# Two moves around layer A's attention in a two-layer decoder trunk: the third pair's loads go behind the last gate product, and a one-column exponential goes among the last projection products

## The chip, the cores and the metric

One core of a Trainium2 chip runs the whole kernel. The metric is device time in microseconds (us), the median of the runs of one kernel. Engines are named as the profile names them: PE (TensorE matmul), PEld (its weight loads), DVE (VectorE), ACT (ScalarE), POOL (GpSimd) and SP (SyncE, which here issues nearly all DMAs).

## The reference, cut to what matters

```python
# layer A (x: 2048 x 1024, 16 heads of 64)
u = rmsnorm(h, norm_a_g);  proj = u @ w_in_a
q, k, v, f_logit, gate = split(proj)              # q, k normed per head
o = fox_attention(q, k, v, log_sigmoid(f_logit + b_forget))   # causal softmax with a forget bias
h = h + (o * silu(gate)) @ w_out_a
# then shared K/V from rmsnorm(h), and layer B: sliding-window attention with sinks,
# again h + (o * silu(gate)) @ w_out_b
```

## The kernel before, in words

Every product with weights is made of three matmuls on pairs of high and low parts (`h`, `lo`), so that it is close to fp32. The core works through four stages: the projections of layer A (`projections`), the attention of layer A (`attention_a`), the output projection (`out_a`), and layer B.

`projections` goes through groups of columns of `w_in_a`; for each block of 128 rows 24 matmuls (L804) fill a PSUM tile `b2` (the trace says `b`), and ACT reads it out (L572 for v, with DVE's L573 behind it). In the last group (the second half of v) the hook runs `attention_a`'s generator a step further between matmuls: 40 such steps (`EARLY`) each put one piece of the row maxima (L982) among the projection products, and step 3 (`REST_AT`) loads the rest of head 0.

`attention_a` then takes steps of two key blocks: scores on PE (L1027, L1028, and masks in L1033 and L1037), exponential on ACT (L1043 or L1034), its split into a high part (ACT, L1046) and a low part (POOL, L1047), sums on DVE (L1056), and the products with v (L1071, in the PSUM tile `pa`). Among these steps PE gets "filler": the gate projection, one matmul (L1117) at a time from the generator `gate`. A gate product is a PSUM tile of 128 features x 512 rows, made of 24 matmuls; its operands are eight pairs of tiles `wh` and `wl`, which hold the normed input of 512 rows, and two tiles of split weights, each 512 KB, loaded from the DRAM scratch `wg` (L1093) into tiles of the tag `wr` (two buffers) or, at the end, alternately of `st` (four buffers) and `wr`. Behind each product come DVE L1129, ACT L1130 (tanh), DVE L1131, and a store to `gt` (L1132). The last 60 matmuls of the filler are kept for the end of attention: 12 finish a product in the bank `pb`, 24 make the next-to-last product in a bank of `mx`, and 24 make the last product in `pb` again. Between them stand the last values' output (L1081, stores to `om` and `oc`) and the reciprocal of the last row sums (`recips`: PE L953, DVE L959 and L960, a store to `rd`).

`out_a` consumes "pairs": a pair is a tile of 128 rows of `o * silu(gate)`, transposed, for two heads and 512 positions. Its four inputs (`om`, `oc`, `gt` and the reciprocal sums `rd`, 256 KB each) are loaded by `gated_load` (L1246 to L1251). For the first three pairs these go to tiles of the tags `qn` (two buffers), `wh`, `qn` and `wl`; for the later ones to `wh`, `wl`, `wh`, `wl`. A pair is then prepared: for pairs 0 and 1 by five operations on POOL (L1263), for the later ones by POOL L1274, DVE L1275 and L1278, ACT L1279 and DVE L1280. Step s of `out_a` is 24 matmuls (L1320) with pair s; `op.step(s)` prepares pair s + 2 and loads up to pair s + 5. Steps 0 and 1 come first for six of the eight bank halves and then for the last two, so step 2 begins behind 48 matmuls.

What sets the order: the code is written in one sequence, and a scheduler with priorities and its own time estimates then orders each engine's instructions; those pinned with `keep_in_program_order` keep their place. A DMA waits at the head of SP's queue for the data or the buffer it needs and holds back every DMA behind it. Buffers are handed round within a tag. The kernel divides PSUM into eight banks; `attention_a` uses `sc` (3), `mx` (2), `pa`, `pb` and `ac`, and `out_a` lays its own tiles over the same banks.

Where ACT goes over to a function of another table, an `ACT_TABLE_LOAD` stands ahead of it in the trace. `constants` makes a one-column tile `warm` and applies a square root to it.

Of the kernel before, what the change touches and what calls it, by code (L numbers as in the profile page):

```python
# [17 lines left out]
AF = mybir.ActivationFunctionType  # L18
# [5 lines left out]
P = 128  # L24
# [45 lines left out]

MAX_AT = 5
EARLY = 40
REST_AT = 3

IDLE = 22
# [28 lines left out]
def f_(ap):  # L104
    return ap.bitcast(F32)
# [57 lines left out]
class Trunk:  # L163
# [57 lines left out]
    def constants(self):  # L221
        nc, cp, a = self.nc, self.const, self.a

        def select(view, src, pattern, base, cm, fill):
            nc.gpsimd.affine_select(
                out=view, in_=src, pattern=pattern, compare_op=ALU.is_ge,
                fill=fill, base=base, channel_multiplier=cm,
            )

        def tile_(name, shape, dt=F32):  # L230
            return cp.tile(shape, dt, name=name, tag=name)

        idle = self.sb("sq", [P, CH], F32R)
        nc.vector.memset(f_(idle), 0.0)
        ps = self.ps("pb", [P, CH])
        for i in range(IDLE):
            self.tc.keep_in_program_order(
                nc.tensor.matmul(ps, idle[:, :P], idle, start=i == 0, stop=i == IDLE - 1)
            )

        self.ones = tile_("ones", [P, P])
        nc.gpsimd.memset(self.ones, 1.0)
        self.tri = tile_("tri", [P, P])
        select(self.tri, self.ones, [[1, P]], 0, -1, 0.0)
        self.ident = tile_("ident", [P, P])
        select(self.ident, self.tri, [[-1, P]], 0, 1, 0.0)

        self.fold = tile_("fold", [P, 32])
        nc.vector.tensor_tensor(self.fold, self.ident[:, :32], self.ident[:, 32:64], ALU.add)
        for c in (64, 96):  # L250
            nc.vector.tensor_tensor(self.fold, self.fold, self.ident[:, c : c + 32], ALU.add)
        nc.vector.tensor_single_scalar(self.fold, self.fold, 2.0, ALU.mult)
        self.identb = tile_("identb", [P, P], BF16)
        nc.vector.tensor_copy(self.identb, self.ident)

        self.mask_s = tile_("mask_s", [P, P], BF16)
        nc.gpsimd.memset(self.mask_s, 0.0)
        select(self.mask_s, self.mask_s, [[1, P]], 0, -1, NEG)

        self.band = tile_("band", [P, 2, P], BF16)  # L260
        nc.gpsimd.memset(self.band[:, 0], 0.0)
        select(self.band[:, 0, :], self.band[:, 0, :], [[-1, P]], 0, 1, NEG)
        nc.vector.tensor_tensor(self.band[:, 1], self.tri, self.ident, ALU.subtract)

        self.loads = []
        warm = tile_("warm", [P, 1])
        nc.scalar.activation(warm, self.ones[:, :1], AF.Sqrt)

        def vector(name, n, views):
            t = tile_(name, [P, n])  # L270
            for rows, src in views:
                self.loads.append((t[rows], src))
            return t

        def column(name, src, n):
            return vector(name, n, [(slice(0, P), src.rearrange("(t p) -> p t", p=P))])

        def pair_column(name, src):
            col = src.rearrange("(p o) -> p o", o=1)
            return vector(name, 1, [(slice(0, HD), col), (slice(HD, P), col)])  # L280

        def row(name, src, n):
            return vector(name, n, [(slice(0, P), src.to_broadcast([P, n]))])

        self.g_a = column("g_a", a["norm_a_g"][0], NDT)
        self.bf = row("bf", a["b_forget"], H)
        self.g_qa = pair_column("g_qa", a["qnorm_a_g"][0])
        self.g_ka = pair_column("g_ka", a["knorm_a_g"][0])
        self.g_b = column("g_b", a["norm_b_g"][0], NDT)
        self.g_kv = column("g_kv", a["kv_norm_g"], NDT)  # L290
        self.g_qb = pair_column("g_qb", a["qnorm_b_g"][0])
        self.g_kb = pair_column("g_kb", a["knorm_b_g"])
        self.sink = row("sink", a["sinks"], H)
        self.gq16 = row("gq16", a["qnorm_b_g"][:, :ROT], ROT)
# [601 lines left out]
    def attention_a(self, op):  # L896


        nc, tc, d = self.nc, self.tc, self.d
# [28 lines left out]
        def load_rest(h):  # L928
            kq = self.sb("big", [P, 2, S], F32R)
            nc.sync.dma_start(out=f_(kq[:, 0, :]), in_=d["ka"][h])  # L930
            nc.sync.dma_start(out=f_(kq[:, 1, :]), in_=d["qa"][h])
            if h % 2 == 0:
                v2 = self.sb("big", [P, 2, NTB, P], F32R)
            else:
                v2 = heads[h - 1][5]
            v = v2[:, h % 2]
            nc.sync.dma_start(out=f_(v), in_=d["va"][h].rearrange("(n p) e -> p n e", p=P))
            heads[h][0], heads[h][2] = kq[:, 0, :], kq[:, 1, :]
            heads[h][4:] = v, v2
# [218 lines left out]
        def ahead(target):  # L1158
            nonlocal done
            while done < min(target, len(pieces)):  # L1160
                pieces[done]()
                done += 1

        for n in range(EARLY):
            yield
            if n == REST_AT:
                load_rest(0)
            ahead(n + 1)
        yield
        pht, plt = self.sb("big", [P, 4, 1024], F32R), self.sb("big", [P, 4, 1024], F32R)  # L1170
# [53 lines left out]
                next(parts)  # L1224
        for _ in op.prepare_parts(1):
            pass
        op.load(2, ("qn", "wh", "qn", "wl"))
        for item, more in zip(pending, HELD):
            feed(fed + more)
            values(item, pin=more > 0)  # L1230
# [6 lines left out]
            op.weight_split(p)  # L1237
        for _ in filler:
            pass


    def gated_load(self, ch, p, tiles):
# [479 lines left out]
```

## Time and profile before

| | |
|---|---|
| median of 3 runs | 2425.08 us (2423.46 to 2425.10) |
| the profiled execution | 2422.62 us |
| its span, first to last instruction | 2420.9 us |
| granted TensorE clock, mean | 0.998 |
| PE busy | 2398.9 us, 99% of the span |
| DVE, ACT, POOL busy | 1731.5, 1259.7, 999.5 us |

The span is shorter than the profiled execution's own time by 1.7 us, which lie around it. Times in the views count from the start of the span. In a row of the timeline stand start, duration, engine, source line, operation, output tile and input tiles; the bracket at the end is the idle time of the engine before this row and what ended it. The rows of the DMA queue (SPq) are the issues, not the transfers. Attention of layer A runs from about 591 to 1449 us, `out_a` from 1449 to 1626 us.

### The profile page before, as it was taken

What the parts mean: (1) busy time and instruction counts of PE and PEld (TensorE: products, weight loads), DVE (VectorE), ACT (ScalarE), POOL (GpSimd) and SP (SyncE); (2) the same over time, 40 slices, a digit from 0 to 9 for tenths busy, and PEclk for the clock granted to TensorE, in tenths of its full rate; (3) what the DMA queues carried; (4) which work ended last, traced back from release to release, by engine and by line L of the source; (5) the groups of instructions that cost most, each with busy time, mean ns of one, the idle gap of its engine ahead of it and who ended that gap; (6) DMA issues with size and microseconds to landing.
All of it is one profiled execution on the core that took longest, in us unless ns stands there. A gap on an engine that the chain in (4) does not pass through costs nothing.

```text
span 2420.9 us, 36284 instructions
## 1 busy us (share of the span) xinstructions
PE 2398.9 (99%) x11960; PEld 2027.5 (84%) x11960; DVE 1731.5 (72%) x4086; ACT 1259.7 (52%) x2502; POOL 999.5 (41%) x644
## 2 busy tenths in 40 slices
PE   9999999999999999999999989999999999999999
PEld 7888899988888888888888868888888888888887
DVE  7756667735898998988989855456766643677775
ACT  5433324323878778878878751135423322466664
POOL 0000000011877777877877862210011000388885
PEclk9999999999999999999999999999999999999999
DMA  6656555677654755575476549975434484765652
GB/s 189 204 170 190 155 152 170 196 230 233 189 159 124 223 135 172 146 228 158 115 215 162 148 131 314 298 261 150 133 97 126 149 265 143 234 219 181 183 183 74
DMA packets 357004, 436.03 MB, mean 180 GB/s; under 512 B 65296, under 2 KB 248624, under 8 KB 350640
## 3 DMA queue, kind: packets, MB, share of 16 engines
q1 hardware_dynamic: 348464, 403.30, 55.3%
q10 hardware_dynamic: 8352, 30.41, 4.3%
q8 instruction: 95, 1.56, 0.3%
q14 instruction: 93, 0.76, 0.1%
HBM read 273.69 MB, written 159.79 MB: 179 GB/s over the span
## 4 chain that ended last, share of the span: by engine, by line
PE 95%; DMA 2%; DVE 1%; POOL 1%; ACT 1%; issue 0%; SPq 0%; POOLq 0%; ACTq 0%
PE b L804 30%; PE pa L1071 10%; PE pb L1549 7%; PE pb L1117 7%; PE sc L1027 5%; PE b L1320 5%; PE sc L1028 5%; PE mx L982 5%; PE b L766 4%; PE b L1403 3%; PE pa L1488 2%; PE pb L766 2%; PE fl L368 1%; PE pa L368 1%; PE pb L368 1%; PE pa L766 1%
## 5 line engine op out<-in xcount | busy, mean ns | idle before, releaser
L804 PE MATMUL b<-wh,big 128*128 128x512 f32 (+3 forms) x2560 | 772.3, 374 | 1.1 <-DVE big L405 0.6
L1047 POOL TENSOR_TENSOR big<-st,big 128x1024 fp32r<-128x1024 f32 (+1 forms) x320 | 657.7, 2077 | 236.5 <-ACT big L1046 162.4
L804 PEld LDWEIGHTS b<-wh,big 128*128 128x128 f32 x2560 | 470.6, 188 | 72.8 <-ACT wh L515 2.5
L804 PE MATMUL b<-wl,big 128*128 128x512 f32 (+3 forms) x1280 | 473.7, 370 | 1.2 <-DVE wl L516 1.1
L1056 DVE TENSOR_TENSOR ac<-ac,st 128x512 f32<-128x512 f32 (+3 forms) x576 | 353.2, 613 | 32.7 <-ACT ac L1050 14.2
L1043 ACT ACTIVATE st<-sc 128x512 f32<-128x512 f32 (+1 forms) x512 | 274.6, 583 | 109.9 <-PE sc L1028 46.2
L1071 PE MATMUL pa<-big 128*128 128x512 f32 (+3 forms) x1280 | 318.5, 365 | 0.8 <-POOL big L1047 0.6
L1046 ACT CAST big<-st 128x1024 fp32r<-128x1024 f32 (+1 forms) x320 | 294.8, 922 | 8.1
L804 PEld LDWEIGHTS b<-wl,big 128*128 128x128 f32 x1280 | 241.3, 189 | 37.2 <-DVE wl L516 5.2
L1071 PEld LDWEIGHTS pa<-big 128*128 128x128 f32 x1280 | 228.9, 190 | 37.1 <-POOL big L1047 1.9
L1027 PE MATMUL sc<-big 128*128 128x512 f32 (+3 forms) x640 | 233.6, 369 | 0.1
L995 DVE TENSOR_REDUCE mt<-mx 128x1 f32<-128x384 f32 (+1 forms) x360 | 214.2, 598 | 27.0 <-PE mx L982 24.6
L524 ACT ACTIVATE sq<-b,r 128x512 f32<-128x512 f32 (+2 forms) x128 | 77.7, 607 | 298.0 <-PE b L804 298.0
L1028 PE MATMUL sc<-big 67*128 67x512 f32 (+3 forms) x640 | 229.2, 367 | 0.0
L982 PE MATMUL mx<-big 66*128 66x512 f32 (+2 forms) x600 | 225.4, 379 | 0.0
L526 DVE TENSOR_REDUCE sm<-sq 128x8 f32<-128x512 f32 (+2 forms) x128 | 74.8, 584 | 138.6 <-ACT sq L524 138.4
L906 POOL MEMSET rot<- 128x512 bf16 x1 | 0.5, 524 | 418.8 <-PE pb L368 418.8
L1117 PE MATMUL pb<-wh,wr 128*128 128x512 f32 x488 | 171.3, 394 | 0.0
L1451 POOL TENSOR_TENSOR big<-big,tri 128x1024 fp32r<-128x1024 f32 x60 | 144.1, 2402 | 61.0 <-DVE big L1448 61.0
L990 DVE CUSTOM_DVE_ANT_0 mx<-mx,rot 128x384 f32<-128x384 f32 (+2 forms) x240 | 147.6, 620 | 27.9 <-PE mx L982 25.2
L1027 PEld LDWEIGHTS sc<-big 128*128 128x128 f32 x640 | 121.5, 190 | 22.6 <-ACT st L1043 1.1
L539 POOL TENSOR_TENSOR ro<-qn,rot 128x64 f32<-128x64 f32 (+1 forms) x48 | 15.6, 325 | 296.4 <-DVE qn L530 290.8
(289 smaller groups left out, 4229.4 us busy)
## 6 DMA issues: line engine op xcount, KB each, us to landing
wr<-wg ACTq DMA_DIRECT2D x58, 512.0 KB
va<-st SPq DMA_DIRECT2D x32, 512.0 KB
ka<-st SPq DMA_DIRECT2D x64, 256.0 KB
ut<-big SPq DMA_DIRECT2D x16, 1024.0 KB
big<-ka SPq DMA_DIRECT2D x16, 1024.0 KB
big<-qa SPq DMA_DIRECT2D x16, 1024.0 KB
qb<-st SPq DMA_DIRECT2D x64, 256.0 KB
big<-qb SPq DMA_DIRECT2D x16, 1024.0 KB
```

Of the source, the lines that this page charges most:

```text
L766: nc.tensor.matmul(ps, W[k][dt][:, ft * P : (ft + 1) * P], u[ch][:, dt, :], start=(dt == 0 and i == 0), stop=(dt == NDT - 1 and i == 2),)
L804: nc.tensor.matmul(ps[:, :n], u[tb // 4][:, dt, us], W[k][dt], start=(dt == 0 and i == 0), stop=(dt == NDT - 1 and i == 2),)
L982: mm = nc.tensor.matmul(ps, qb[:66, i * P : (i + 1) * P], kb[:66, k0:k1], start=True, stop=True,)
L995: nc.vector.reduce_max(o, ps, axis=AX.X)
L1027: nc.tensor.matmul(o, ka[:, ks], qa[:, qs], start=not (last and n_), stop=False)
L1028: nc.tensor.matmul(o, kb[:, ks], qb[:, qs], start=False, stop=not diag)
L1043: nc.scalar.activation(pf[:, off : off + w], ps[:, :w], AF.Exp, scale=HD**-0.5)
L1046: nc.scalar.copy(ph[:, :tw], pf[:, :tw])
L1047: nc.gpsimd.tensor_tensor(pl[:, :tw], pf[:, :tw], f_(ph[:, :tw]), ALU.subtract)
L1056: nc.vector.tensor_tensor(a_, a_, pf[:, off : off + w], ALU.add)
L1071: product = nc.tensor.matmul(pv[:, q0 : q0 + w], v[:, k, :], src[:, off : off + w], start=(p == 0 and n_ == 0 and i == 0), stop=(last and ...
L1117: nc.tensor.matmul(ps, w[:, dt // 2 % 2, wk, dt % 2, :], us[dt][uk], start=(dt == 0 and i == 0), stop=(dt == NDT - 1 and i == 2),)
```

## The change

A load of the third pair (`op.load(2, ...)`, five DMAs) moves from ahead of the last products of attention to behind the last gate product; and in step 20 of the 40 early steps a one-column exponential on `warm` is issued and pinned, among the last projection products. `warm` becomes an attribute for that. Nothing that reaches the output is computed otherwise.

```diff
+EXP_AT = 20
...
-        warm = tile_("warm", [P, 1])
-        nc.scalar.activation(warm, self.ones[:, :1], AF.Sqrt)
+        self.warm = tile_("warm", [P, 1])
+        nc.scalar.activation(self.warm, self.ones[:, :1], AF.Sqrt)
...
             if n == REST_AT:
                 load_rest(0)
+            if n == EXP_AT:
+                exp = nc.scalar.activation(self.warm, self.ones[:, :1], AF.Exp)
+                tc.keep_in_program_order(exp)
             ahead(n + 1)
...
         for _ in op.prepare_parts(1):
             pass
-        op.load(2, ("qn", "wh", "qn", "wl"))
         for item, more in zip(pending, HELD):
             feed(fed + more)
             values(item, pin=more > 0)
         gate_bank, weight_slots = "mx", cycle(["st", "wr"])
         feed(fed + 3 * NDT)
         gate_bank = "pb"
         for _, args in due:
             recips(*args)
         for p in range(PAIRS_READY):
             op.weight_split(p)
         for _ in filler:
             pass
+        op.load(2, ("qn", "wh", "qn", "wl"))
```

Since the scheduler orders the instructions, the diff doesn't show the new order. Lines of the kernel before stand one to four lower in the changed one (L1093 is L1094, L1132 is L1133, L1246 is L1250, L1275 is L1279). First SP's queue at the end of attention, from the third last load of gate weights (`wr<-wg`) to the store of the last reciprocal sums or beyond; before:

```order
L1093 DMA wr<-wg 128x1024
L1093 DMA st<-wg 128x1024
L1247 DMA wh<-oc 128x512
L1251 DMA wl<-rd 64x512
L1246 DMA qn<-om 128x512
L1248 DMA qn<-gt 128x512
L1251 DMA wl<-rd 64x512
L1083 DMA om<-sq 64x512
L1132 DMA gt<-sq 128x512
L1084 DMA oc<-sq 64x512
L1093 DMA st<-wg 128x1024
L1093 DMA wr<-wg 128x1024
```

and the same place of the changed kernel, up to the third pair's last load:

```order
L1094 DMA wr<-wg 128x1024
L1094 DMA st<-wg 128x1024 x2
L1094 DMA wr<-wg 128x1024
L1084 DMA om<-sq 64x512
L1085 DMA oc<-sq 64x512
L1133 DMA gt<-sq 128x512
L1250 DMA qn<-om 128x512
L1251 DMA wh<-oc 128x512
L1252 DMA qn<-gt 128x512
L1255 DMA wl<-rd 64x512
L962 DMA rd<-sq 48x32
L1255 DMA wl<-rd 64x512
```

The last two loads of gate weights stood behind the third pair's five loads and three stores; they now stand ahead of all of them.

Then DVE behind the next-to-last gate product (whose bank is `mx`), up to the third pair's last operation; `sq_15306`/`sq_15298` belong to the last gate product, `qn_15190`/`qn_15303` to the third pair, `wh_15322`/`wh_15323` to the fourth. Before:

```order
L1129 TENSOR_TENSOR sq_15306<-pb_15277,rows_13561 128x512
L1275 TENSOR_TENSOR wh_15322<-wh_15322,wl_15325 128x512
L1131 SCALAR_TENSOR_TENSOR sq_15306<-sq_15306,pb_15277 128x512
L1275 TENSOR_TENSOR qn_15190<-qn_15190,wl_15193 128x512
L1278 TENSOR_TENSOR wh_15322<-wh_15322,wh_15324 128x512
L1278 TENSOR_TENSOR qn_15190<-qn_15190,qn_15192 128x512
L1280 TENSOR_TENSOR big_14360<-wh_15322,big_14360 128x512
L1280 TENSOR_TENSOR big_14360<-qn_15190,big_14360 128x512
```

and now:

```order
L1130 TENSOR_TENSOR sq_15298<-pb_15269,rows_13562 128x512
L1132 SCALAR_TENSOR_TENSOR sq_15298<-sq_15298,pb_15269 128x512
L1279 TENSOR_TENSOR qn_15303<-qn_15303,wl_15306 128x512
L1282 TENSOR_TENSOR qn_15303<-qn_15303,qn_15305 128x512
L1279 TENSOR_TENSOR wh_15323<-wh_15323,wl_15326 128x512
L1284 TENSOR_TENSOR big_14361<-qn_15303,big_14361 128x512
```

The third pair still comes behind the last gate product; one operation of the fourth pair, which waits for that pair's loads, stands ahead of the third pair's last.

Last ACT at the step from the projections (L572, each on the next tile `b2`) to attention (L1043); before:

```order
L572 ACTIVATE st_5576<-b2_5529,r_144 128x8x64
L572 ACTIVATE st_5620<-b2_5580,r_144 128x8x64
L572 ACTIVATE st_5664<-b2_5624,r_144 128x8x64
L572 ACTIVATE st_5713<-b2_5668,r_144 128x8x64
L1043 ACT_TABLE_LOAD
L1043 ACTIVATE st_5726<-sc_5724 128x512
```

and now:

```order
L1170 ACT_TABLE_LOAD
L1170 ACTIVATE warm_132<-ones_108 128x1
L573 ACTIVATE st_5577<-b2_5529,r_144 128x8x64
L573 ACTIVATE st_5621<-b2_5581,r_144 128x8x64
L573 ACTIVATE st_5665<-b2_5625,r_144 128x8x64
L573 ACTIVATE st_5714<-b2_5669,r_144 128x8x64
L1044 ACTIVATE st_5727<-sc_5725 128x512
```

The table load stands four projection products earlier, and none is left ahead of attention's first exponential.

## The prediction

> **What bounds the kernel now.** I read the page first, then the waits of PE, then the timelines of the two places that the change touches. The page's rows of busy time:
>
> ```profile
> span 2420.9 us, 36284 instructions
> PE 2398.9 (99%) x11960; PEld 2027.5 (84%) x11960; DVE 1731.5 (72%) x4086; ACT 1259.7 (52%) x2502; POOL 999.5 (41%) x644
> ```
>
> PE is busy for 99% of the span, so a change that leaves the matmuls alone can only win what PE waits or runs slowly. The waits of PE, the longest and the two that matter beside it (total, times, longest):
>
> ```profile
> PE pb L1117 <- DMA st<-wg: 11.3, 1, 11.3
> ...
> PE b L804 <- DVE big L405: 0.6, 1, 0.6
> PE pa L1071 <- POOL big L1047: 0.6, 2, 0.4
> ```
>
> One wait of 11.3 us is most of what PE loses: the last gate product waits for its first weights. SP's timeline tells why they came late:
>
> ```profile
> 1419.45 0.33 SPq L1093 DMA_DIRECT2D wr<-wg  x1
> 1419.89 0.36 SPq L1093 DMA_DIRECT2D st<-wg  x1
> 1426.81 0.32 SPq L1247 DMA_DIRECT2D wh<-oc  x1
> ...
> 1431.77 0.33 SPq L1246 DMA_DIRECT2D qn<-om  x1
> 1433.11 0.32 SPq L1248 DMA_DIRECT2D qn<-gt  x1
> 1433.48 0.48 SPq L1251 DMA_DIRECT2D wl<-rd  x1
> ...
> 1434.69 0.54 SPq L1132 DMA_DIRECT2D gt<-sq  x1
> ...
> 1435.83 1.44 SPq L1093 DMA_DIRECT2D st<-wg  x1
> 1437.36 0.38 SPq L1093 DMA_DIRECT2D wr<-wg  x1
> ...
> 1452.20 0.54 SPq L1246 DMA_DIRECT2D wh<-om  x1
> ```
>
> From 1420.3 to 1435.8 the queue holds the third pair's loads, and three of them go out right behind an operation of pair 1 on POOL, whose buffers they need (the last row quoted is the first load of pair 5, used further down):
>
> ```profile
> 1417.12 7.43 POOL L1047 TENSOR_TENSOR big<-st,big 128x1024 fp32r<-128x1024 f32 x3 [0.48 <-ACT big L1046]
> 1424.52 2.27 POOL L1263 TENSOR_TENSOR qn<-qn,wh 128x512 f32<-128x512 f32 x1
> ...
> 1430.48 1.26 POOL L1263 TENSOR_TENSOR qn<-qn 128x512 f32<-128x512 f32 x1
> 1431.82 1.26 POOL L1263 TENSOR_TENSOR big<-qn,big 128x512 fp32r<-128x512 f32 x1
> ```
>
> L1247 follows the operation that ends at 1426.79, L1246 the one that ends at 1431.74, L1248 the one that ends at 1433.08. The gate weights need none of these; they only stand behind. PE's rows there:
>
> ```profile
> 1423.86 0.40 PE L1117 MATMUL pb<-wh,wr 128*128 128x512 f32 x1
> ...
> 1424.89 0.44 PE L1117 MATMUL mx<-wh,st 128*128 128x512 f32 x1
> ...
> 1430.52 0.28 PE L953 MATMUL sc<-fold,part 128*48 128x32 f32 x2
> 1442.09 0.76 PE L1117 MATMUL pb<-wh,st 128*128 128x512 f32 x1 [11.30 <-DMA st<-wg]
> ...
> 1448.98 8.32 PE L1320 MATMUL b<-big 128*128 128x512 f32 x36
> ...
> 1459.86 4.24 PE L1320 MATMUL b<-big 128*128 128x512 f32 x18
> ...
> 1465.30 4.24 PE L1320 MATMUL b<-big 128*128 128x512 f32 x18
> ```
>
> **Term 1, the wait.** In the changed order both loads of last gate weights stand ahead of the third pair. The `st` load follows its predecessor at once: of the four `st` buffers it takes the one of the third last attention step, whose POOL reader is the first of the three L1047 from 1417.12; a third of 7.43 us later is 1419.6. So it goes out at about 1420.3. The chain of waits shows what such a load took with others around it:
>
> ```profile
> 1435.83 6.13 DMA st<-wg
> ```
>
> At 6.13 us it lands by 1426.4, and PE wants it at 1430.8, when L953 ends. The `wr` load waits for the matmul at 1423.86, goes out at 1424.3 and lands by 1430.4; its 12 matmuls begin half a product later, at 1433.5. The bank `pb` must be read out first, which DVE's L1131 ends at 1429.86 (row below). All 11.30 us go.
>
> **Term 2, the clock.** The windows (length, busy times by engine, granted clock, DMA share, GB/s) of the last gate product, of the products behind it, and of a long stretch of the output projection:
>
> ```profile
> 1442.10:1449.00 6.90, 6.90 (x25) 5.60 (x26) 0.00 (x0) 0.00 (x0) 1.28 (x1) 0.79 0.74 218
> 1449.00:1454.40 5.40, 5.40 (x25) 4.49 (x24) 5.13 (x7) 1.45 (x3) 1.62 (x1) 1.00 0.70 200
> ...
> 1459.90:1481.00 21.10, 21.10 (x95) 17.48 (x94) 11.65 (x15) 5.32 (x7) 4.40 (x3) 1.00 1.03 346
> ```
>
> After its wait PE runs the product at a granted clock of 0.79 on the mean. Its 24 matmuls take 1448.98 - 1442.09 = 6.89 us; 24 of the output projection take 1465.30 - 1459.86 = 5.44. Without the wait there is no reason for the slow clock: 1.45 us more. [...]
>
> **Term 3, crowding.** The earlier `st` load now flies beside the two issued at 1419.45 and 1419.89, and PE takes the second of these at 1424.89. The window of those two:
>
> ```profile
> 1419.90:1424.40 4.50, 4.39 (x20) 3.29 (x19) 4.43 (x6) 3.25 (x5) 4.50 (x2) 1.00 0.72 235
> ```
>
> They move 235 x 4.5 = 1.06 MB and so end by about 1424.4. Shared evenly, 0.52 MB more at the 346 GB/s of a saturated stretch take 1.5 us, so the next-to-last product could wait until 1425.7, 0.8 us. Served in turn it waits not at all. I take 0.2 us of loss, near the end without a wait, since two loads issued 0.44 us apart already landed in time for PE here. [...]
>
> **Term 4, the exponential.** ACT and PE at the start of attention, and windows there:
>
> ```profile
> 591.65 0.69 ACT L572 ACTIVATE st<-b,r 128x512 fp32r<-128x512 f32 x1 [6.02 <-PE b L804]
> 592.36 1.28 ACT L1043 ACT_TABLE_LOAD   x1
> 593.65 0.60 ACT L1043 ACTIVATE st<-sc 128x512 f32<-128x512 f32 x1
> ...
> 590.00:600.00 10.00, 9.39 (x45) 7.11 (x45) 4.02 (x10) 8.32 (x14) 3.84 (x3) 1.00 0.83 250
> ```
>
> The table load of 1.28 us stands ahead of the first exponential and so of the split, POOL's part and the first products with v. But PE has other matmuls: of these 10 us it lacks 0.61, 0.4 of it in the wait for POOL. The gain is bounded by 0 and 0.61; the scheduler also moves a few gate matmuls here, so I take the middle, 0.3. The load's new place costs nothing: the last L572 finds ACT idle for 6.02 us, as long as a projection product takes, and 1.28 us and one column of exponential fit. If that cover were gone, PE would be late by at most 1.3 us.
>
> **What else is moved.** The stores to `om`, `oc` and `gt` go out ahead of the third pair, when their data is there. The third pair's loads still wait for POOL: L1250 at 1431.8, L1252 at 1433.1. Behind them stands the new neighbour, the store of the last reciprocal sums, and the third pair's last load is queued behind that. DVE's rows:
>
> ```profile
> 1429.17 0.69 DVE L1131 SCALAR_TENSOR_TENSOR sq<-sq,pb 128x512 f32<-128x512 f32 x1 [0.70 <-ACT sq L1130]
> 1438.47 0.69 DVE L1129 TENSOR_TENSOR sq<-mx,rows 128x512 f32<-128x512 f32 x1 [8.62 <-DMA gt<-sq]
> ...
> 1454.86 0.69 DVE L1280 TENSOR_TENSOR big<-qn,big 128x512 fp32r<-128x512 f32 x1
> ```
>
> The `gt` store issued at 1434.69 released DVE at 1438.47, 3.8 us. Issued at 1429.9 it releases its buffer by 1433.7, and the reciprocals follow to 1434.3; then go the `rd` store, the last `rd` load at 1434.8 and, from 1435.7, pair 3. The output projection can start at 1448.98 - 12.75 = 1436.2. Pair 2 is needed 10.88 us later (1459.86 - 1448.98), at 1447.1. DVE does the last gate product's part to about 1438.7, then pair 2 and, ahead of its last operation, one of pair 3, whose last load is issued at 1438.5. At 3.8 us of landing this ends about 1443.5; at 6.13 about 1446. Before, it ended at 1455.55, 4.3 us early; now 1 to 3.6. No wait, but the cover is thin. For the later pairs the loads come some 2.5 us later against PE than before (pair 5: issued 3.2 us behind the projection's start, now 5). Their cover before, by the two rows with the least of it that I found:
>
> ```profile
> 1487.34 1.63 DVE L1280 TENSOR_TENSOR big<-wh,big 128x512 fp32r<-128x512 f32 x1 [0.69 <-ACT big L1279]
> ...
> 1496.69 1.46 DVE L1280 TENSOR_TENSOR big<-wh,big 128x512 fp32r<-128x512 f32 x2
> ```
>
> Steps 9 and 10 begin at 1459.86 + 7 x 5.44 = 1497.9 and at 1503.4; their pairs end at 1489.0 and 1497.4, so 9 and 6 us remain, and about 6 and 3.5 after the change. At the start of layer B DVE's L405 goes ahead of two operations of the projection's end, and ACT's order changes; PE's wait of 0.6 for that L405 can go or grow to about twice that: 0, with 0.6 either way.
>
> **The sum**: 11.30 + 1.45 - 0.2 + 0.3 = 12.85 us. The profiled execution took 2422.62 us, of which 1.7 lie around the span; it would take 2409.8. It was 2.46 us faster than the median, so I forecast 2425.08 - 12.85 = 2412.2 us, 0.53% less.
>
> **Rivals.** (a) Pair 2 comes late, and a part of the wait moves into the output projection. For it speaks DVE's new order, behind a load of pair 3; against it the 1 to 3.6 us left. If DMAs there take 10 us, pair 2 ends near 1450 and PE waits 3 us: 2415. If later pairs lose their cover too, say 3 us more, 2418. (b) The output projection falls to the pace of its loads, and the time ends on the other side: the loads of pairs 2 to 4 flew during the wait, and behind it DMA is full (share 1.03). Three pairs of 1.05 MB at 346 GB/s are 9 us, which leaves 3.9 us of gain; it is slower than before only from 12.85 us of loss, and by 0.2% from 17.7, which is six pairs' loads with no cover at all: 2430. Against it stand 6 to 9 us of cover and three pairs, not six. (c) The change doesn't do what it says: the gate weights still land late, because a buffer or the crowd holds them. Only a landing time above 10.5 us for `st` (1420.3 to 1430.8) or 9.2 for `wr` makes PE wait; at 12 us some 3 us return: 2415. (d) The exponential does nothing: 2412.5, within the range.
>
> **How the numbers follow.** Forecast with (d) 0.82, (a) 0.10, (c) 0.04, (b) 0.04, of which slower than before 0.015. The forecast's own range is the sum with its ends: gain 11.30 + 1.45 - 0.8 + 0 - 0.6 = 11.35 to 11.30 + 1.45 + 0.6 + 0.6 = 13.95, so 2411.1 to 2413.7; the three runs differ by 1.6 us, and the profiled one lies lower still, so 2409.5 to 2415. For 8 in 10 I add most of (a): 2409 to 2417. A difference under 0.2% (4.85 us) can't be told from none; all of the forecast and most of (a) and (c) lie beyond it: faster 0.95, same 0.03, slower 0.02.
>
> **What the changed profile would show.** PE's wait for `st<-wg` gone, the clock 1.00 through the last gate product, the output projection starting at about 1436, `st<-wg` issued twice in a row near 1420, no `ACT_TABLE_LOAD` between 592 and 594, and L1320 without a gap. A wait of PE on DVE's L1284 at step 2, or of the next-to-last gate product for `st<-wg`, would show terms wrong; a gap in steps 9 to 12 would show (b).

## The result: 12.4 us faster, as forecast, with a small loss in the output projection

The changed kernel takes 2412.66 us (median of 5 runs, 2411.01 to 2414.55) against 2425.08 for the kernel before (5 runs, 2422.65 to 2426.01). The ratio is 0.995, 95% interval 0.9937 to 0.9963, so 9 to 15 us less. The forecast was 2412.2. Measured a second time, beside new runs of the kernel before, it took 2411.59 against 2423.43 (ratio 0.9948, 0.9936 to 0.996).

Here is the changed kernel's profile. First the page's span and busy times, then PE's waits (total, times, longest):

```profile
span 2408.8 us, 36281 instructions
PE 2399.6 (100%) x11960; PEld 2026.4 (84%) x11960; DVE 1732.4 (72%) x4086; ACT 1260.6 (52%) x2503; POOL 1000.6 (42%) x644
...
PE pb L239 <- DVE sq L235: 1.5, 1, 1.5
PE pa L426 <- DVE ro L413: 0.7, 2, 0.4
PE b L1324 <- DVE big L150: 0.7, 1, 0.7
```

PE's busy time is 0.7 us longer and the span 12.1 us shorter, so in sum what went is waiting. (The last gate product got 1.31 us shorter, as worked out further down, but PE's busy time in the output projection grew by 0.88 us and that at the head of attention by 0.5.) The wait for `st<-wg` is gone. One in the list is new, 0.7 us for DVE's L150 (the low part of a block of the output projection's weights). SP's timeline at the end of attention:

```profile
1418.69 0.33 SPq L1094 DMA_DIRECT2D wr<-wg  x1
1419.13 1.12 SPq L1094 DMA_DIRECT2D st<-wg  x2
1423.52 0.32 SPq L1094 DMA_DIRECT2D wr<-wg  x1
...
1429.12 0.33 SPq L1133 DMA_DIRECT2D gt<-sq  x1
1431.02 0.33 SPq L1250 DMA_DIRECT2D qn<-om  x1
...
1435.11 0.38 SPq L1250 DMA_DIRECT2D wh<-om  x1
...
1442.28 0.54 SPq L1250 DMA_DIRECT2D wh<-om  x1
...
1458.78 0.58 SPq L140 DMA_DIRECT2D st<-in_w_out_a  x1
```

Both `st` loads go out in a row at 1419.13, and the `gt` store is 5.6 us earlier than before, when it stood behind the third pair (1434.69). The row at 1442.28 is the first load of pair 5, and the last row loads a block of the output projection's weights; before, the load of the same block was this row:

```profile
1466.61 0.58 SPq L139 DMA_DIRECT2D st<-in_w_out_a  x1
```

PE and DVE of the changed kernel at the end of attention and in the output projection:

```profile
1424.14 0.50 PE L1118 MATMUL mx<-wh,st 128*128 128x512 f32 x1
...
1430.05 0.50 PE L1118 MATMUL pb<-wh,st 128*128 128x512 f32 x1
...
1435.63 8.32 PE L1324 MATMUL b<-big 128*128 128x512 f32 x36
...
1446.51 4.24 PE L1324 MATMUL b<-big 128*128 128x512 f32 x18
...
1469.55 1.66 PE L1324 MATMUL b<-big 128*128 128x512 f32 x6 [0.72 <-DVE big L150]
...
1429.95 0.69 DVE L1130 TENSOR_TENSOR sq<-mx,rows 128x512 f32<-128x512 f32 x1 [0.86 <-PE mx L1118]
...
1443.54 0.69 DVE L1284 TENSOR_TENSOR big<-qn,big 128x512 fp32r<-128x512 f32 x1
```

No bracket stands behind 1424.14 or 1430.05: neither gate product waits. DVE's first part of the next-to-last product (1429.95) now follows PE; before it waited 8.62 us for a `gt` store. Pair 2 is ready at 1444.23 and wanted at 1446.51. The windows of the last gate product, of the start of attention, and of the whole output projection after; and, as a fourth row, the output projection before:

```profile
1430.00:1436.00 6.00, 6.00 (x28) 4.96 (x28) 1.72 (x4) 0.63 (x1) 2.69 (x3) 1.00 0.66 202
590.00:600.00 10.00, 9.90 (x50) 7.41 (x50) 4.09 (x10) 7.72 (x15) 4.41 (x3) 1.00 0.81 253
1435.60:1611.50 175.90, 175.18 (x775) 144.13 (x774) 94.19 (x126) 29.36 (x46) 40.10 (x30) 1.00 0.96 299
...
1449.00:1623.30 174.30, 174.30 (x775) 144.42 (x774) 94.56 (x127) 32.19 (x50) 37.04 (x28) 1.00 0.95 294
```

The clock is 1.00 through the last gate product. The output projection, which had no wait before, is 1.5 us longer. ACT's rows ahead of PE's wait of 0.72 us show the cast of the late block of weights (L149), right behind the cast of a pair (L1283) that had itself waited:

```profile
1466.66 0.62 ACT L1283 CAST big<-wh 128x512 fp32r<-128x512 f32 x1 [4.92 <-DVE wh L1282]
1467.19 1.05 ACT L149 CAST big<-st 128x1024 fp32r<-128x1024 f32 x1
```

The exponential with its table load stands in ACT's timeline so:

```profile
565.17 1.28 ACT L1170 ACT_TABLE_LOAD   x1
566.47 0.20 ACT L1170 ACTIVATE warm<-ones 128x1 f32<-128x1 f32 x1
571.12 0.69 ACT L573 ACTIVATE st<-b,r 128x512 fp32r<-128x512 f32 x1 [4.44 <-PE b L805]
```

ACT then still stands idle for 4.44 us, so the load costs nothing at its new place. The marks of the account are the starts of these PE rows; first those of before (the first scores; the last group of the output projection), then those of after:

```profile
591.45 0.39 PE L1027 MATMUL sc<-big 128*128 128x512 f32 x1
...
1623.28 0.85 PE L1320 MATMUL pb<-big 128*128 128x512 f32 x3
```

```profile
590.74 0.39 PE L1028 MATMUL sc<-big 128*128 128x512 f32 x1
...
1611.48 0.86 PE L1324 MATMUL pb<-big 128*128 128x512 f32 x3
```

| stretch | before | after | gained |
|---|---|---|---|
| start to the first scores | 591.45 | 590.74 | 0.71 |
| first scores to the next-to-last gate product | 833.44 | 833.40 | 0.04 |
| from there to the start of the output projection | 24.09 | 11.49 | 12.60 |
| output projection, to its last group | 174.30 | 175.85 | -1.55 |
| from there to the end | 797.62 | 797.32 | 0.30 |
| span | 2420.9 | 2408.8 | 12.10 |

### The profile page after: what moved, and what is told of

Read it like the earlier page. It is cut to its first block, busy times and chain, and to the rows that moved or that the text cites. A ratio compares the mean times of both kernels' runs of the same rounds, so it can differ in the third digit from the quotient of the medians.

```text
span 2408.8 us, 36281 instructions
## 1 busy us (share of the span) xinstructions
PE 2399.6 (100%) x11960; PEld 2026.4 (84%) x11960; DVE 1732.4 (72%) x4086; ACT 1260.6 (52%) x2503; POOL 1000.6 (42%) x644
## 4 chain that ended last, share of the span: by engine, by line
PE 95%; DMA 2%; DVE 1%; ACT 0%; issue 0%; SPq 0%; POOL 0%; DVEq 0%; ACTq 0%; POOLq 0%
PE b L805 32%; PE pa L1072 11%; PE pb L1118 7%; PE pb L1553 7%; PE sc L1028 5%; PE sc L1029 5%; PE mx L983 5%; PE b L1324 4%; PE b L767 4%; PE b L1407 2%; PE pa L1492 2%; PE pb L767 2%; PE fl L369 1%; PE pa L369 1%; PE pb L369 1%; PE pa L767 1%
## 5 line engine op out<-in xcount | busy, mean ns | idle before, releaser
L1029 PEld LDWEIGHTS sc<-big 67*128 67x128 f32 x640 | 121.9, 190 | 18.8
```

Of the source, the lines that this page charges most:

```text
L1029: nc.tensor.matmul(o, kb[:, ks], qb[:, qs], start=False, stop=not diag)
```

## The experiments

All have intervals against the kernel before, run between them on the same chip. For each the table gives the two stretches in which something moved, from its own profile by the marks above.

| kernel | ratio, 95% interval | gate products to projection | output projection |
|---|---|---|---|
| before | | 24.09 | 174.30 |
| the change | 0.995, 0.9937 to 0.9963 | 11.49 | 175.85 |
| the change, again | 0.9948, 0.9936 to 0.996 | 11.45 | 176.72 |
| e1, loads alone | 0.9947, 0.9934 to 0.9959 | 11.45 | 175.23 |
| e2, exponential alone | 0.9996, 0.9987 to 1.0005 | 24.95 | 174.29 |
| e3, weights on ACT's queue | 0.9968, 0.9956 to 0.9981 | 11.45 | 180.89 |
| e4, wait filled, 46 wide matmuls | 1.0021, 1.0012 to 1.003 | 22.22 | 183.23 |
| e5, projection's weights first | 0.9957, 0.9944 to 0.9969 | 11.45 | 175.57 |
| e6, loads between the products | 0.9999, 0.999 to 1.0008 | 24.50 | 174.29 |
| e7, the change, weights on ACT's queue | 0.9966, 0.9954 to 0.9979 | 11.44 | 177.43 |
| e8, wait filled, 100 small matmuls | 1.0029, 1.0019 to 1.0039 | 32.30 | 174.29 |
| e9, as e5 | 0.9952, 0.9938 to 0.9965 | 11.49 | 177.14 |

**e1 and e2: one half of the change each.** e1 is the changed kernel without this piece:

```diff
-            if n == EXP_AT:
-                exp = nc.scalar.activation(self.warm, self.ones[:, :1], AF.Exp)
-                tc.keep_in_program_order(exp)
```

> The loads moved, without the exponential. The theory (terms 1 and 2: the last gate weights no longer stand behind the third pair's loads in SP's queue, and PE keeps its full clock) expects that PE's wait for st<-wg goes, that the stretch from the start of the next-to-last gate product to the start of the output projection takes 11.5 us as in the changed kernel (24.1 before), and 12.0 to 12.6 us off the time. The rival, that the early table load has a share in the gain beyond its 0.3 us, expects less than 11.5 us.

e2 has the exponential, and `op.load(2, ...)` back where it stood before.

> The exponential alone, with the third pair's loads in their old place. Term 4 expects PE's busy time from 590 to 600 us up by 0.3 to 0.5 us, no table load between 592 and 594 us, the wait of 11.3 us for st<-wg still there, and a time 0 to 0.4 us below that of the kernel before. The rival (d) expects that attention makes the head start good: its end comes at the same distance from its start less 0 us, and the time is the same within 0.2 us. The comparison of times can hardly tell these apart; the rows at the start and the end of attention can.

e1 took 2411.62 us beside 2423.91, 12.3 less: all that can be measured of the change is the loads. e2 took 2423.49, 0.4 less, and its interval holds 1. Its window at the start of attention, and its last gate product, which comes after a wait of 10.97 us:

```profile
590.00:600.00 10.00, 9.90 (x51) 7.58 (x49) 3.98 (x9) 7.14 (x13) 3.83 (x3) 1.00 0.80 252
```

```profile
1441.60:1449.70 8.10, 8.10 (x25) 6.44 (x26) 0.00 (x0) 0.00 (x0) 1.28 (x1) 0.67 0.77 235
```

PE's busy time rises from 9.39 to 9.90 us as term 4 said. But from the first scores to the next-to-last gate product e2 takes 1424.74 - 591.33 = 833.41 us, against 833.44. So in this pair of executions what is won at the head of attention is not seen at its end. One pair can't settle it, though: leaving out e1 and e3, whose attention holds further waits, and taking e7's wait of 0.77 us off, this stretch takes 833.27 to 833.77 us with the exponential and 833.44 to 833.52 without, a spread wider than the term. Neither term 4 nor rival (d) is shown.

**e3 and e7: the same loads from another queue.** Both issue the last product's two weight loads from ACT, whose queue holds nothing else there; e3 leaves the rest as before, e7 has the change as well.

```diff
-                            w = loads.pop(n) if n in loads else gate_weights(n)[0]
+                            late_ = nc.scalar if n >= groups - 2 else nc.sync
+                            w = loads.pop(n) if n in loads else gate_weights(n, late_)[0]
```

> The third pair's loads stay ahead as before, but the two loads of the last gate weights go out from ACT's queue instead of SP's. If the 11.3 us were the place behind the third pair's loads in SP's queue (the theory), the weights go out at about 1421 and 1426 us, PE's wait for st<-wg goes or is below 1 us, and the time falls by 10 to 13 us, although nothing is moved in the order of the work. If instead a buffer, or the crowd of the third pair's transfers, held the weights, the wait stays at 5 us or more, and the time falls by less than 7 us.

> The changed kernel, with the two loads of the last gate weights on ACT's queue, so that the last product's first load flies beside the next-to-last one's first load from another queue, and nothing else of the third pair is near. In the changed kernel both stood in one queue, and the next-to-last product did not wait (term 3 came out as 0). If loads of one queue are served in turn but loads of two queues share the DMA engines evenly, the next-to-last product now waits 0.5 to 1 us for st<-wg, as it did (0.79) when the third pair's loads were still ahead, and its load takes 5.5 to 6.2 us from issue to PE. If that wait of 0.79 us came from somewhere else, for one from the third pair's loads in SP's queue, it is gone here (below 0.1 us). The time is 11.5 to 12.5 us below the kernel before.

e3 came out 7.9 us faster (2416.03), between the 10 to 13 us of the theory and the 7 us of its rival, and its rows tell why. Its issues (ACT's two, then SP's `gt` store), PE and DVE:

```profile
1420.76 0.33 ACTq L1093 DMA_DIRECT2D st<-wg  x1
...
1425.88 0.33 ACTq L1093 DMA_DIRECT2D wr<-wg  x1
...
1434.74 0.54 SPq L1133 DMA_DIRECT2D gt<-sq  x1
...
1426.61 0.50 PE L1118 MATMUL mx<-wh,st 128*128 128x512 f32 x1 [0.79 <-DMA st<-wg]
...
1432.49 0.50 PE L1118 MATMUL pb<-wh,st 128*128 128x512 f32 x1
...
1441.24 7.09 PE L1321 MATMUL b<-big 128*128 128x512 f32 x30 [1.65 <-DVE sq L1132]
...
1438.75 0.69 DVE L1130 TENSOR_TENSOR sq<-mx,rows 128x512 f32<-128x512 f32 x1 [8.87 <-DMA gt<-sq]
```

The wait ahead of the last product is gone with the third pair's loads still ahead in SP's queue: no buffer and no crowd held the weights, only their place. But the `gt` store still stands behind those loads. DVE waits 8.87 us for it (8.62 before), reads the next-to-last product's bank late, and the output projection, which now comes 11 us sooner, waits 1.65 us for that bank. That store was the next thing to be late, hidden before by the longer wait. PE waits 2.9 us more further on in e3's projection (for a pair, a split of weights and a bank that DVE reads out); what holds those back was not followed. In e7 the scheduler put the third pair's loads ahead of the stores again, and PE waits 1.2 us for the same bank and 0.9 us for pair 2, so its 9.1 us do not reach the 11.5 expected.

Both answer term 3. In e7 the next-to-last product's load left SP at 1419.86 with the last product's `st` load beside it from ACT at 1419.94; PE waited for it until 1425.78, 5.9 us (the third pair's first load left at 1425.76, behind both). In the changed kernel the two left one queue in a row from 1419.13, and PE took the first at 1424.14, 5.0 us later, without a wait. e7's two issues and PE's row:

```profile
1419.86 0.36 SPq L1094 DMA_DIRECT2D st<-wg  x1
...
1419.94 0.33 ACTq L1094 DMA_DIRECT2D st<-wg  x1
...
1425.78 0.50 PE L1119 MATMUL mx<-wh,st 128*128 128x512 f32 x1 [0.77 <-DMA st<-wg]
```

From two queues, in e7, the loads share, and the loss of 0.77 us is the 0.8 that the prediction gave for an even share; from one queue, in the changed kernel, the first is served first. The two kernels differ in one thing more: the second load leaves 0.08 us behind the first in e7 and 0.8 us behind it in the changed kernel. But the semaphore updates that mark the landing of each load speak for the queue: in the changed kernel those of the second load (1424.4 to 1425.3) begin after the last of the first (1423.3 to 1424.1), and in e7 the two overlap (1424.9 to 1425.7 and 1425.2 to 1426.1).

**e4 and e8: keeping PE busy through the wait.** Both are the kernel before with matmuls on a spare bank ahead of the last gate product; their result is read by nobody. The edit in e4's form:

```diff
+        spare = self.ps("sc", [P, CH])
+        for i in range(DUMMY):            # e4: 46, of 512 columns; e8: 100, of 8
+            tc.keep_in_program_order(
+                nc.tensor.matmul(
+                    spare, op.y(0)[:, 0, :P], op.y(0)[:, 0, :],
+                    start=i == 0, stop=i == DUMMY - 1,
+                )
+            )
```

> Everything as before, but 46 matmuls on a spare bank, whose result nobody reads, fill PE's wait of 11.3 us ahead of the last gate product (46 at 0.23 us are 10.6 us). The wait as such stays. Term 2 (the clock falls because PE stands still) expects the last gate product at a granted clock of 1.00 and 5.4 to 5.6 us long instead of 6.89, and 1.3 to 1.5 us off the time. The rival (the product is slow because its weights or the busy DMA hold it) expects 6.5 us or more and a time within 0.5 us of the kernel before.

> The wait of 11.3 us again kept busy, now by 100 matmuls of 8 columns, which leave the order of every other engine's instructions as in the kernel before (46 of 512 columns had changed it). They take some 7 to 10 us. Term 2 expects that the last gate product follows at a clock of 1.00 in 5.4 to 5.6 us if they reach to within 2 us of its start, and that the time then falls by 1.2 to 1.5 us, since nothing else is moved. If the 4.8 us lost with the wide matmuls were the work of a busy PE and not of the changed order, the time is 2 us or more above the kernel before.

e4's window of the last gate product, and its longest waits of PE:

```profile
1440.80:1446.30 5.50, 5.47 (x24) 4.59 (x25) 0.00 (x0) 0.00 (x0) 0.00 (x0) 1.00 0.86 286
```

```profile
PE b L1329 <- DVE big L1340: 3.1, 1, 3.1
PE pb L1329 <- DVE sq L1132: 1.7, 1, 1.7
...
PE b L1329 <- ACT big L1288: 1.2, 1, 1.2
```

At a clock of 1.00 the product takes 1446.36 - 1440.83 = 5.53 us, with its weights still late (PE begins it at 1440.83) and the DMA busier (0.86): its slowness was the clock, as term 2 has it. The time as a whole rose by 4.8 us all the same. The scheduler, which counts the 46 matmuls as work, put three weight loads and two of `in_x` (512 KB each) ahead of the rest of the fourth pair's loads. One of the fourth pair's operations stands ahead of the last product's L1132 on DVE, as in the kernel before, and now comes late. Of PE's waits in the projection, 1.7 us are for this L1132 and 1.2 for a pair; the longest, 3.1 us, is for a bank that DVE reads out (L1340), and its cause was not followed. So e4 shows the term, and its time shows nothing about it.

e8 was to repeat this with every other engine's order unchanged. Its windows, the first three from the start of the small matmuls, the fourth that of the last gate product:

```profile
1430.60:1434.00 3.40, 3.40 (x33) 3.40 (x31) 0.00 (x0) 0.00 (x0) 2.26 (x2) 1.00 0.37 95
1434.00:1437.00 3.00, 3.00 (x16) 3.00 (x15) 0.00 (x0) 0.00 (x0) 1.27 (x1) 0.50 0.89 254
...
1441.00:1448.00 7.00, 7.00 (x35) 7.00 (x35) 0.00 (x0) 0.00 (x0) 0.00 (x0) 0.50 0.26 95
...
1448.80:1457.00 8.20, 8.20 (x25) 6.54 (x26) 0.00 (x0) 0.00 (x0) 1.27 (x1) 0.65 0.63 175
```

It missed: 2431.37 us, 6.8 above the kernel before. PE never stands still in these rows, and yet after 3.4 us the clock falls to 0.50; the 100 matmuls take 18.4 us instead of the 7 to 10 expected and the product behind them 8.20. In the kernel before, where PE stands idle from 1430.8, the clock falls at nearly the same time (1.00 from 1433 to 1434 us, 0.87 in the next us, then 0.50): the small matmuls held the clock no longer than standing still did. The output projection keeps its 174.29 us, so what e8 loses lies ahead of it (32.30 us in the table for 24.09), and e4's loss in the projection is not of that kind.

**e5 and e9: a candidate.** The changed kernel, with the projection's weight load of a step written ahead of the pairs' loads of that step:

```diff
+        if s + NDT // 2 < NDT:
+            self.weight_load(s + NDT // 2)
...
-        if s + NDT // 2 < NDT:
-            self.weight_load(s + NDT // 2)
```

> The changed kernel, with the loads of the output projection's weights issued ahead of the pairs' loads of the same step. If the changed kernel's wait of 0.72 us at step 6 for the split of such weights comes from their load standing behind the pairs' loads, it goes, and the time is 0.5 to 0.8 us below the changed kernel's. If the loads as a whole are too slow for the projection (rival (b)), the wait goes over to the pairs: PE waits 0.5 us or more for DVE's last operation on a pair, and the time is the same or longer.

> The changed kernel with the output projection's weights ahead of the pairs' loads, a second time. Its first profile had no wait for the weights' split but came into attention 1.8 us later than the changed kernel's, with 2.4 us of PE's waits for ACT in the projections. If those belong to the execution and not to the order (which is the same up to the output projection), attention starts within 0.5 us of the changed kernel's 590.8 and the time is 0.5 us or more below it; if they belong to this build, attention starts at 592 us or later again and the time stays at 2412.9.

PE's largest wait in the output projection of e9, and in e5's the same line:

```profile
1482.10 5.03 PE L1324 MATMUL b<-big 128*128 128x512 f32 x18 [1.91 <-DVE big L1335]
```

```profile
1481.80 5.02 PE L1324 MATMUL b<-big 128*128 128x512 f32 x18 [0.32 <-DVE big L1335]
```

The wait for the weights' split is gone in both, and a wait for DVE's L1335 (which reads out a bank of the projection) takes its place: DVE's order had changed with the loads', and in e9 that L1335 stands behind an L1279 which waits 2.46 us for a pair's last load. e5 took 2412.93 and e9 2413.51 us, no better than the change. e9 came into attention at 591.26, so the late start of e5 (592.59) belonged to its execution, but the time did not fall as that half expected. No version here beats the changed kernel; e1 can't be told from it.

**e6: the loads one product earlier than in the change.** `op.load(2, ...)` is written between the next-to-last and the last gate product.

> The third pair's loads written between the next-to-last and the last gate product, halfway between the two versions. The scheduler then still issues them ahead of the last two loads of gate weights. The theory expects a wait for st<-wg of 8 to 11 us still there and a time within 3 us of the kernel before. If it were enough to issue these loads later, whatever stands behind them, half of the wait or more would go and the time fall by 6 us or more.

```profile
PE pb L1118 <- DMA st<-wg: 10.5, 1, 10.5
```

```profile
1435.84 0.60 SPq L1094 DMA_DIRECT2D st<-wg  x1
```

2423.47 us beside 2423.43: nothing gained. The scheduler still issues the third pair ahead of the weights, and the last product's first load leaves when it did before (1435.84 for 1435.83). That the loads are written later wins nothing as long as they stay ahead of the weights in the queue.

## Why the prediction was right, term by term

- **Term 1, the wait, and the place in the queue: right.** The 11.30 us are gone. With after's 0.71 us earlier start taken off, the issues were forecast to 0.4 us (the second of the two in the row at 1419.13 left at 1419.93, for 1420.3; the `wr` load at 1423.52, for 1424.3), the start of the output projection to 0.2 (1435.63 for 1436.2). e3 shows the cause by itself, e6 from the other side. Rival (c) is out.
- **Term 2, the clock: right in kind, its size unsteady.** The product fell from 6.89 to 5.58 us (1435.63 - 1430.05), 1.31 for 1.45. Where the wait stays, the product took 6.89, 8.11 (e2: 1449.69 - 1441.58) and 8.08 us (e6: 1449.41 - 1441.33) in three executions, so the term is worth 1.3 to 2.5 us from one to the next. In all three the product takes its first matmuls slowly: full clock came back about 2.9 us (before: 0.50 until 1445.0 us, then 1.00) and 5.4 us (e2 and e6, with 0.67 on the mean over the product) behind the product's start, by windows of a quarter of a us. What sets that point no run here shows.
- **Term 3, crowding: 0, for 0.2 taken.** The forecast weighed 0.8 (shared) against 0 (in turn). Both were seen: in turn from one queue (the changed kernel, where PE does not wait), shared from two (e7, where it waits 0.77 us). The working of the 0.8 doesn't close (1424.4 + 1.5 is 1425.9, not 1425.7, and 1.0 us behind 1424.89), so that e3 and e7 lose just 0.8 is in part luck.
- **Term 4, the exponential: not seen at the end of attention.** At the head the gain is there: in the window from 590 to 600 us PE is busy 0.51 us longer, and in the first 15 us of attention, counted from the first scores, it is busy 14.38 to 14.40 us in the five profiles without the exponential and 14.66 to 14.79 in the seven with it, the 0.3 us of the term. The step took this for a gain of the whole; in the profiled pair 0.04 us of it (0.03 in e2) was left at the end of attention. PE has no wait there that would say where the rest went, and the spread of that stretch (e2, above) is too wide to tell 0.3 from nothing.
- **What else is moved: the pairs held, the weights did not.** Pair 2 was ready 2.3 us ahead, inside the 1 to 3.6 forecast, so rival (a) did not come. But "L1320 without a gap" failed. The step looked for cover at the pairs alone. It also put the later loads 2.5 us later against PE than before, and they came later than that: pair 5 is issued 6.65 us behind the projection's start (3.2 before, 5 forecast). The loads of `w_out_a` stand in the same queue behind the pairs'; the one issued at 1458.78 left 23.15 us behind the projection's start, for 17.63 before (1466.61 - 1448.98). Its cast on ACT then stood behind that of a pair, so PE waited 0.72 us for its split, and with what PE loses around that the projection gave back 1.55 us. This is rival (b) in its place and in a small size: 0.9 us (e1), 1.55 here and 2.4 in the second run of the change, not the 9 that it priced.
- **Start of layer B:** the wait for L405 is gone, and from the projection's last group on 0.30 us are gained, within the 0.6 allowed.

By the profiled pair, 12.60 + 0.04 - 1.55 + 0.30 = 11.4 us come from the change, for 12.85 forecast; 0.71 us more came from the projections of layer A, where no work was changed but the place of the exponential, and where attention's first scores start anywhere from 590.10 (e1) to 592.59 (e5). A wait of PE of 0.94 us at 39.6 us, which only the profile of the kernel before has, is one such difference. So the sum missed by 1.4 us in these two executions, most of it in the output projection. The medians differ by 12.4; that the 6.89 us of the product before were the shortest of three seen can account for up to 1.2 us of this, but with runs that spread by 3 us it stays open. That the forecast of 2412.2 lies within 0.5 us of the median is therefore in part luck: a loss of 1.55 us that it had at nothing was made up by differences that it had not foreseen either.

## What to carry to other kernels

When PE waits for a load, look at the issue time first: if the load went out late, read what stands ahead of it on its queue, and for which buffer each of these waits. A move that frees one load should free the stores behind the same blockers too (in e3 and e7, where the `gt` store stayed behind, PE waits 1.65 and 1.2 us for the bank that it holds back), and the order that counts is the scheduled one, not the written one (e6, e7). After a long wait is taken out, count the cover of every stream that used it to run ahead, weights as well as data.

## What was not expected of the hardware

- PE lost its clock while the profile calls it busy: with matmuls of 8 columns back to back it fell from 1.00 to 0.50 after 3.4 us (e8), while 46 matmuls of 512 columns kept it at 1.00 (e4). No idle time of PE stands in the profile there. Whether their width or the weight load ahead of each sets this was not tried.
- A `gt` store released DVE 3.8 us after its issue in the kernel before; in the changed kernel the one issued at 1429.12 had released it by 1431.25, 2.1 us. The DMA was less busy around the second (share 0.34 from 1429.12 to 1431.2 us) than around the first (0.83 from 1434.69 to 1438.4); whether that is the reason was not tried.
- Two loads of 512 KB issued close together reached PE at different times: the first of two from one queue within 5.0 us (the changed kernel), from two queues after 5.9 us (e7; in e3 PE waited 0.79 us for it as well), though in e7 the second also left sooner behind the first (0.08 us for 0.8).
